# Split-weight buffers in the feed-forward blocks of a streaming encoder step: eleven slots in order of use instead of two big pairs and a ring of three

## The chip, the cores and the metric

The kernel runs on one core of a Trainium2 chip. Its engines are PE (the matrix engine, with PEld for its weight loads), DVE (vector), ACT (scalar), POOL (GpSimd) and SP, which here only issues DMA transfers. Every engine takes its instructions in the order in which they stand in its queue, and waits on semaphores for the others. The metric is the device time of one execution in microseconds (us).

## What is computed

One inference step of a two-layer encoder trunk: 512 frames of a new stream and 8 x 16 frames of running streams (640 columns in all), width 1024. Layer 0 is a convolution module, layer 1 is chunked attention over a shared K/V. Each is followed by a SwiGLU feed-forward block of hidden width 2816, and these two blocks are what the change touches.

```python
def swiglu_ffn(h, g, w_in, w_out):
    a, b = jnp.split(rms_norm(h, g) @ w_in, 2, axis=-1)
    return h + (jax.nn.silu(a) * b) @ w_out

def run_trunk(x, ...):                       # for the prompt and for the sample group
    for l in range(DEPTH):                   # DEPTH = 2
        if l < N_A_LAYERS:
            h, st = conv_module(h, ...)      # GLU, causal depthwise conv of width 31, LayerNorm, swish
        else:
            if l == N_A_LAYERS:
                k, v = jnp.split(rms_norm(h, norm_kv) @ w_kv, 2, axis=-1)
            q = rms_norm(h, norm_attn[j]) @ w_q[j]
            h = h + attention(q, k, v, rel_bias[j]) @ w_o[j]
        h = swiglu_ffn(h, norm_ffn[l], w_ffn_in[l], w_ffn_out[l])
    return rms_norm(h, norm_final), new_hist, k, v
```

All values are float32. The outputs are the two normed streams, the convolution buffers and the K and V rows.

## The kernel before

**Precision.** A float32 value is cut into a high and a low part, both of the matmul type fp32r: ACT copies the value (`hi`), DVE subtracts that copy from it (`lo`). In the feed-forward block `cut` (through `put`, lines 319 and 320) does this for weights. A product then takes three matmuls for each 128 x 128 piece of weights: hi by hi, lo by hi, hi by lo (`product`, line 379).

**Seven products.** `ffn` handles the 640 columns as two halves of 320 (`NH`) and the 1024 inputs as two halves as well. Of 22 blocks of the input matrix (128 gate and 128 value columns each), three (`w_std`, `std`) take the ordinary eight products. The other 19, and 12 blocks of the output matrix, take seven products instead of eight: the four quarters of a block's weights are added up in a fixed pattern (`w_seven`), the activations too (the tiles named X11 to X22), and each of the seven weight combinations meets one activation combination. A product of an input block has 12 matmuls (84 in a block), one of an output block has 9 (63 in a block). The order of work of a layer is: the three ordinary blocks, then three chunks, each of six input blocks (three in the first) followed by four output blocks (`out_chunk`), then four input blocks whose hidden values meet the rest of the output matrix (`w_out`) in ordinary products. In the text an *input block* and an *output block* are these, and an *out chunk* is the four output blocks.

**A block's way.** `w_seven` loads one block: SP issues the load of a 128 x 512 piece into `s1` and of the whole block (128 x 2048 floats, 1 MB; 1536 for an output block) into `raw`. POOL issues two DMAs that add another quarter onto `s1` and onto one quarter of `raw`. ACT and DVE cut the quarters and sums. PE uses the cut weights. `raw` and `s1` have two buffers each.

**Where cut weights stood.** The first four (X11, X21, XT2, XT1) stood together in one big pair `whi`, `wlo` of 2048 columns, of which there are two, used in turn by block. X11 and X21 were cut in one pass over 1024 columns (768 for an output block). The other three (XT3, XT4, X22) stood in a ring of three pairs `shi`, `slo` of 512 columns.

**What sets the order.** The tile framework's scheduler orders each engine's queue at build time, by the program's order and by priorities: weight cuts and the copies out of PSUM are marked as urgent (`tc.high_priority`). The products of an out chunk follow a string, `QORD`: in "51" the 5 is the product (`prod` in `out_chunk`) and the 1 the output block; "a0" and "a1" are the last two products (XT4 and X22) of the input block ahead, which `seven` hands on as `after`. So the last two products of each input block come after the first ones of the next block.

**Copies out of PSUM.** `keep` (line 388) is an ACT copy of a partial sum before the next product is added to the same PSUM tile, `plus` (line 393) is a DVE addition, and line 508 adds an output product to the residual `h` on DVE.

The lines that the prediction uses: 356 and 357 (SP loads of `s1` and `raw`), 361 and 362 (POOL's adding DMAs), 319 and 320 (cuts), 364 and 370 (sums of quarters on DVE), 379 (matmuls), 388 and 393 (copies and additions from PSUM), 604 (loads of `w_out`).

## Time and profile before

| what | value |
|---|---|
| three runs | 1534.5, 1539.4 and 3146.81 us; median 1539.4 us |
| the profiled execution | 1537.75 us, span 1535.9 us, granted TensorE clock 0.983 |
| PE busy | 1456.9 us (95%) |
| DVE busy | 1082.2 us (70%) |
| ACT busy | 739.7 us (48%) |
| feed-forward block of layer 0 | about 267 us to 676 us of the span; 326 to 664 us lies inside its seven-product part |
| feed-forward block of layer 1 | about 1082 us to 1517 us of the span; 1144 to 1478 us lies inside its seven-product part |

The rest of the span is the convolution module (up to 267 us) and attention (about 676 to 1082 us). A row of a wait list names who waited, on which line, and for whom, then the sum in us, the number of waits and the longest one. A row of a window list names a stretch of the span and then, by engine, busy time and number of instructions, after these the granted TensorE clock (1.00 is full) and the mean busy share of the DMA engines. Since matmuls overlap, the matrix engine counts as busy when it could have started another matmul: its busy share is no measure of how fast matmuls follow each other.

### The profile page before, as it was taken

The numbers are of one execution on the slowest core, as the hardware profiler recorded it, in microseconds if no ns is written. First come the engines' busy times: TensorE is split into PE (matmuls) and PEld (weight loads), VectorE is DVE, ScalarE is ACT, GpSimd is POOL, SyncE is SP. The second block draws the span as 40 slices with busy tenths as digits, with TensorE's granted clock in tenths as the row PEclk, the third lists the DMA queues.
The fourth block names the chain that finished last, engine by engine and source line by source line (L and its number), as shares of the span: only waits on it lengthen the run. The fifth ranks groups of instructions, "written<-read, shape, count | busy, mean of one in ns | idle before, by whom it ended". The sixth has DMA issues, their size and how long they took to land.

```text
span 1535.9 us, 28172 instructions
## 1 busy us (share of the span) xinstructions
PE 1456.9 (95%) x10974; PEld 1376.3 (90%) x10974; DVE 1082.2 (70%) x2357; ACT 739.7 (48%) x1555; POOL 337.9 (22%) x374
## 2 busy tenths in 40 slices
PE   5999899999999999999999999978999999999995
PEld 5998689999999999999887888957999999999994
DVE  5789346788688677676676666654788678688664
ACT  3666246453453553455564453542554454454442
POOL 5789222011111111113221121111001111111101
PEclk9999899999999999999999999998999999999997
DMA  7267414146655655534565455541235665665521
GB/s 235 63 188 181 100 56 137 42 97 146 155 136 142 157 134 127 152 117 146 189 190 189 139 173 192 172 154 42 69 72 136 152 149 127 156 147 134 146 90 69
DMA packets 79941, 207.25 MB, mean 135 GB/s; under 512 B 12992, under 2 KB 37312, under 8 KB 71360
## 3 DMA queue, kind: packets, MB, share of 16 engines
q1 hardware_dynamic: 61664, 175.78, 35.6%
q0 software_dynamic: 17856, 29.37, 12.5%
q8 instruction: 86, 1.41, 0.4%
q14 instruction: 47, 0.39, 0.1%
q10 hardware_dynamic: 288, 0.31, 0.1%
HBM read 193.82 MB, written 11.61 MB: 134 GB/s over the span
## 4 chain that ended last, share of the span: by engine, by line
PE 46%; DMA 22%; DVE 17%; ACT 6%; POOL 5%; issue 3%; SPq 0%; POOLq 0%; DVEq 0%; ACTq 0%
PE mm L379 13%; DMA raw<-in_w_in 9%; PE mm L167 8%; PE mm L168 7%; PE mm L169 7%; DMA raw<-in_w_os 6%; DVE wlo L320 4%; DMA s<-in_w_in 4%; POOL ca L726 4%; ACT whi L319 4%; DVE slo L320 3%; PE mm L764 2%; DVE raw L364 2%; DVE h L508 1%; PE w L203 1%
## 5 line engine op out<-in xcount | busy, mean ns | idle before, releaser
L379 PE MATMUL mm<-XH,whi 128*128 128x320 f32 x736 | 223.3, 312 | 8.9 <-ACT whi L319 8.9
L379 PE MATMUL mm<-XH,wlo 128*128 128x320 f32 x736 | 227.8, 311 | 1.3 <-DVE wlo L320 1.3
L379 PE MATMUL mm<-XL,whi 128*128 128x320 f32 x736 | 226.4, 310 | 0.0
L320 DVE TENSOR_TENSOR wlo<-raw,whi 128x1024 fp32r<-128x1024 f32 (+3 forms) x140 | 127.5, 917 | 124.1 <-ACT whi L319 123.9
L167 PE MATMUL mm<-xh,whi 128*128 128x320 f32 (+2 forms) x640 | 200.8, 316 | 4.3 <-ACT xh L156 2.6
L168 PE MATMUL mm<-xh,wlo 128*128 128x320 f32 (+2 forms) x640 | 200.0, 313 | 0.6 <-DVE wlo L151 0.6
L319 ACT ACTIVATE whi<-raw 128x1024 fp32r<-128x1024 f32 (+3 forms) x140 | 113.0, 814 | 178.5 <-DMA raw<-in_w_in 75.9
L169 PE MATMUL mm<-xl,whi 128*128 128x320 f32 (+2 forms) x640 | 197.1, 312 | 0.0
L379 PE MATMUL mm<-XH,shi 128*128 128x320 f32 x504 | 156.1, 310 | 3.7 <-ACT t L388 3.2
L379 PE MATMUL mm<-XH,slo 128*128 128x320 f32 x504 | 155.0, 308 | 0.0
L379 PE MATMUL mm<-XL,shi 128*128 128x320 f32 x504 | 154.4, 308 | 0.1
L379 PEld LDWEIGHTS mm<-XH,whi 128*128 128x128 f32 x736 | 137.1, 189 | 11.1 <-ACT whi L319 11.0
L319 ACT ACTIVATE shi<-raw 128x512 fp32r<-128x512 f32 (+1 forms) x192 | 110.9, 582 | 69.0 <-PE mm L379 61.4
L379 PEld LDWEIGHTS mm<-XH,wlo 128*128 128x128 f32 x736 | 138.8, 189 | 2.6 <-DVE wlo L320 2.4
L379 PEld LDWEIGHTS mm<-XL,whi 128*128 128x128 f32 x736 | 138.5, 189 | 0.0
L379 PE MATMUL mm<-hid,whi 128*128 128x320 f32 x576 | 135.2, 309 | 0.6 <-ACT whi L319 0.6
L320 DVE TENSOR_TENSOR slo<-raw,shi 128x512 fp32r<-128x512 f32 (+1 forms) x192 | 121.2, 635 | 11.3 <-ACT shi L319 10.8
L167 PEld LDWEIGHTS mm<-xh,whi 128*128 128x128 f32 x640 | 121.4, 190 | 7.8 <-ACT xh L156 3.1
L168 PEld LDWEIGHTS mm<-xh,wlo 128*128 128x128 f32 x640 | 121.7, 190 | 1.2 <-DVE wlo L151 0.8
L169 PEld LDWEIGHTS mm<-xl,whi 128*128 128x128 f32 x640 | 120.8, 190 | 1.2 <-issue 1.0
L379 PE MATMUL mm<-hid,shi 128*128 128x320 f32 x432 | 106.7, 312 | 2.9 <-ACT shi L319 1.6
L379 PEld LDWEIGHTS mm<-XH,shi 128*128 128x128 f32 x504 | 94.5, 187 | 6.2 <-ACT t L388 5.6
(228 smaller groups left out, 3503.3 us busy)
## 6 DMA issues: line engine op xcount, KB each, us to landing
raw<-in_w_in SPq DMA_DIRECT2D x38, 1024.0 KB
raw<-in_w_os SPq DMA_DIRECT2D x24, 768.0 KB
cache<-in_ck SPq DMA_DIRECT2D x32, 512.0 KB
cache<-in_cv SPq DMA_DIRECT2D x32, 512.0 KB
raw<-in_w_pw SPq DMA_DIRECT2D x12, 1024.0 KB
s<-in_w_in SPq DMA_DIRECT2D x38, 256.0 KB
s<-in_w_in POOLq DMA_DIRECT2D x38, 256.0 KB, 4.7
raw<-in_w_in POOLq DMA_DIRECT2D x38, 256.0 KB, 4.2
```

The costliest lines, as they stand in the source:

```text
L167: nc.tensor.matmul(ps, wh, xh, start=(i == 0), stop=False)
L168: nc.tensor.matmul(ps, wl, xh, start=False, stop=False)
L169: nc.tensor.matmul(ps, wh, xl, start=False, stop=(i == last))
L203: nc.tensor.matmul(st[:, 512 + t * w + k:513 + t * w + k], s[:, a:a + P], onec, start=True, stop=True)
L319: nc.scalar.activation(out=hi, in_=src, func=AF.Copy)
L320: nc.vector.tensor_tensor(out=lo, in0=src, in1=hi.bitcast(F32), op=sub)
L364: nc.vector.tensor_tensor(out=a11, in0=s1, in1=a11, op=add)
L379: nc.tensor.matmul(pt, wt, v, start=(first and k == i == 0), stop=(k == len(xs) - 1 and i == 2), skip_group_check=True)
L508: nc.vector.tensor_tensor(out=hv, in0=hv, in1=pt, op=sub if row else add)
L726: nc.gpsimd.tensor_tensor(out=acc, in0=acc, in1=pr, op=ALU.add)
L764: nc.tensor.matmul(pt[32 * q:32 * q + 32, 0:n], w4[0:r, 4 * tg + q, :], mv, start=(tg == 0), stop=(tg == 7))
```

## The change

In the feed-forward blocks the two big pairs are allocated once per layer, and the three ring pairs and the eight quarters of the big pairs make a list of eleven slots of 512 columns. `slot()` hands them out in turn. `w_seven` takes one slot per product, in the order in which the products use them, and cuts each product's weights by itself: X11 and X21 are now two passes of 512 columns (384 for an output block) where one pass of 1024 (768) was. The order of the cuts in an output block becomes XT1, X11, X21, XT2, X22, XT3, XT4. In `QORD` product 2 of output block 1 ("21") comes two places later, "61" and "70" change places, and so do "52" and "40". The ordinary blocks and `w_out` use the same memory as before, now by way of the list or of the fixed pairs. No arithmetic changes.

```diff
-QORD = "50 a0 10 a1 20 51 11 21 60 30 61 70 31 52 40 71 12 22 41 62 32 53 72 13 23 42 63 33"
+QORD = "50 a0 10 a1 20 51 11 60 30 21 70 61 31 40 52 71 12 22 41 62 32 53 72 13 23 42 63 33"
...
-        def wbig():
-            return [wp.tile([P, 2048], F32R, tag="w" + t, name=nm("w" + t)) for t in ("hi", "lo")]
-
-        def wring():
-            return [wx.tile([P, 512], F32R, tag="s" + x, name=nm("s" + x), bufs=3)
-                    for x in ("hi", "lo")]
+        wbig = [[wp.tile([P, 2048], F32R, tag="w" + t, name=nm("w" + t)) for t in ("hi", "lo")]
+                for _ in range(2)]
+        slots = [(wx.tile([P, 512], F32R, tag=f"shi{i}", name=nm("shi"), bufs=1),
+                  wx.tile([P, 512], F32R, tag=f"slo{i}", name=nm("slo"), bufs=1), 0)
+                 for i in range(3)]
+        slots += [(hi, lo, o) for hi, lo in wbig for o in range(0, 2048, 512)]
+        turn = [0]
+
+        def slot():
+            turn[0] += 1
+            hi, lo, o = slots[(turn[0] - 1) % len(slots)]
+            return (hi, lo), o
...
             n = src.shape[-1] // 4
-            raw, w = wraw(), wbig()
+            raw, ws = wraw(), {}
...
-            ws = {X11: (w, n), X21: (w, 0), XT2: (w, 2 * n), XT1: (w, 3 * n)}
             with tc.high_priority(offset=HP):
                 nc.gpsimd.dma_start(s1, src[:, 3 * n:4 * n], accum_op=add)
                 nc.gpsimd.dma_start(a21, src[:, n:2 * n], accum_op=add)
-                cut(w, 0, raw[:, :2 * n])
-                nc.vector.tensor_tensor(out=a11, in0=s1, in1=a11, op=add)
-                cut(w, 2 * n, a11)
-                cut(w, 3 * n, s1)
-                for x in (X22, XT3, XT4) if out else (XT3, XT4, X22):
-                    ws[x] = (wring(), 0)
-                    if x == X22:
+                for x in ((XT1, X11, X21, XT2, X22, XT3, XT4) if out else
+                          (X11, X21, XT2, XT1, XT3, XT4, X22)):
+                    if x == XT2:
+                        nc.vector.tensor_tensor(out=a11, in0=s1, in1=a11, op=add)
+                    elif x == X22:
                         nc.vector.tensor_tensor(out=a12, in0=a12, in1=a11, op=add)
-                    cut(*ws[x], {X22: a12, XT3: a21, XT4: a22}[x])
+                    ws[x] = slot()
+                    cut(*ws[x], {XT1: s1, X11: a11, X21: a12, XT2: a11, X22: a12, XT3: a21,
+                                 XT4: a22}[x])
             return ws
...
-            raw, w = wraw(), wbig()
+            raw, w = wraw(), wbig[m0 // 4]
```

What this does to the queues is shown at three places. The first is the ACT queue in layer 0, where two input blocks meet in the middle of the second chunk. Rows of line 319 are cuts (or, with `hid`, hidden values), `whi` and `shi` are slots, the number behind `raw` tells the blocks apart; lines 388 and 397 are a PSUM copy and a SiLU (392 and 401 after the change). In brackets are the semaphores that a row waits for: `DMAHW` is a load by SP, `DMASW` one of POOL's adding DMAs. Before:

```order
L319 ACTIVATE shi_599_4642<-raw_595_4627 128x512 [waits DMASW6_49,Activation_49]
L388 ACTIVATE t1_607_4669<-mm_605_4655 128x320 [waits PE_49]
L319 ACTIVATE hid_590_4581<-B01_580_4530 128x320 [waits DVE_49]
L319 ACTIVATE whi_614_4763<-raw_613_4762 128x1024 [waits DMAHW6_49]
L397 ACTIVATE t1_607_4669<-t1_607_4669 128x320 [waits DVE_49]
L319 ACTIVATE shi_601_4646<-raw_595_4627 128x512 [waits PE_49,Activation_49]
L319 ACTIVATE whi_614_4763<-raw_613_4762 128x512 [waits DVE_49]
L319 ACTIVATE hid_559_4393<-B00_608_4683 128x320 [waits DVE_49]
L319 ACTIVATE shi_603_4650<-raw_595_4627 128x512 [waits PE_49,Activation_49]
```

The ACT queue after the change, at the place that answers to it in the same chunk, where one input block follows another (`raw_525`, then `raw_535`):

```order
L319 ACTIVATE shi_325_2803<-raw_525_4696 128x512 [waits PE_49]
L319 ACTIVATE hid_487_4339<-B00_520_4617 128x320 [waits DVE_49]
L319 ACTIVATE whi_317_2795<-s1_526_4697 128x512 [waits DMASW7_49,PE_49]
L401 ACTIVATE t2_512_4537<-t2_512_4537 128x320 [waits DVE_49]
L392 ACTIVATE t2_522_4666<-mm_517_4589 128x320 [waits PE_49,Activation_49]
L319 ACTIVATE whi_317_2795<-raw_525_4696 128x512
L319 ACTIVATE whi_319_2797<-raw_535_4833 128x512 [waits DMAHW7_49,PE_49]
L319 ACTIVATE hid_490_4374<-B00_520_4617 128x320 [waits DVE_49]
L392 ACTIVATE t1_529_4732<-mm_527_4718 128x320 [waits PE_49]
L319 ACTIVATE shi_321_2799<-raw_535_4833 128x512 [waits DMASW1_49,Activation_49]
```

Before, the last two cuts of a block (of `raw_595`) stood behind the first cut of the next block, which waits for that block's load. After, all cuts of a block (`raw_525`) stand ahead of the first cut of the next one.

The second place is the SP queue in layer 0, from the first out chunk to the input blocks behind it. `s1` and `raw` are the two loads of a block, `in_w_os` are output blocks, `in_w_in` input blocks; a wait for DVE is one for the last cut or sum that read the buffer. Before:

```order
L357 DMA raw_490_3892<-in_w_os0 128x1536 [waits DMAHW4_49,DMASW6_49,DVE_49]
L356 DMA s1_519_4117<-in_w_os0 128x384 [waits DMASW7_49,DVE_49,Activation_49]
L357 DMA raw_503_4003<-in_w_os0 128x1536 [waits DMAHW2_49,DMAHW6_49,DMASW0_49,DVE_49]
L356 DMA s1_532_4218<-in_w_in0 128x512 [waits DMASW1_49,DMAHW3_49,DVE_49,Activation_49]
L357 DMA raw_516_4114<-in_w_os0 128x1536 [waits DMAHW0_49,DMASW2_49,DVE_49]
L356 DMA s1_548_4338<-in_w_in0 128x512 [waits DMAHW5_49,DMASW3_49,DVE_49]
L357 DMA raw_529_4215<-in_w_in0 128x2048 [waits DMAHW2_49,DMASW4_49,DVE_49]
L357 DMA raw_545_4335<-in_w_in0 128x2048 [waits DMAHW4_49,DMAHW7_49,DMASW6_49,DVE_49]
```

After (the loads of `raw` are on line 362 now, those of `s1` on line 361):

```order
L361 DMA s1_464_3984<-in_w_os0 128x384 [waits DMASW5_49,DVE_49]
L362 DMA raw_463_3983<-in_w_os0 128x1536 [waits DMAHW5_49,DMASW7_49,DVE_49]
L361 DMA s1_469_4079<-in_w_os0 128x384 [waits DMAHW2_49,DMASW1_49,DVE_49]
L362 DMA raw_468_4078<-in_w_os0 128x1536 [waits DMAHW3_49,DMAHW6_49,DMASW0_49,DVE_49]
L361 DMA s1_474_4174<-in_w_in0 128x512 [waits DMASW2_49,DVE_49]
L361 DMA s1_482_4288<-in_w_in0 128x512 [waits DMASW4_49,DVE_49,Activation_49]
L362 DMA raw_473_4173<-in_w_in0 128x2048 [waits DMAHW1_49,DMASW3_49,DVE_49]
L362 DMA raw_481_4287<-in_w_in0 128x2048 [waits DMAHW3_49,DMAHW7_49,DMASW5_49,DVE_49]
```

Each `raw` load still waits on DVE for its buffer. The loads of `s1` stand no longer strictly one block ahead: the one of the first input block (`s1_474`) now stands behind the load of the last output block (`raw_468`), where it stood ahead of it.

The third place is PE in the first out chunk of layer 0, where `slo`, `shi`, `whi`, `wlo` are the weight slots and `hid` the hidden values. Before:

```order
L379 MATMUL mm_475_3806<-hid_484_3868,shi_469_3793 128x320 [waits DVE_49]
L379 MATMUL mm_479_3835<-hid_482_3864,whi_466_3779 128x320 [waits DVE_49]
L379 MATMUL mm_501_3931<-hid_482_3864,whi_491_3893 128x320
L379 MATMUL mm_500_3920<-hid_397_3315,shi_494_3907 128x320 [waits Activation_49]
L379 MATMUL mm_479_3835<-hid_399_3320,shi_471_3798 128x320 [waits DVE_49]
```

After:

```order
L383 MATMUL mm_447_3811<-hid_450_3840,shi_325_2803 128x320 [waits DVE_49]
L383 MATMUL mm_461_3901<-hid_450_3840,whi_319_2797 128x320
L383 MATMUL mm_465_4005<-hid_389_3252,shi_325_2803 128x320 [waits Activation_49]
L383 MATMUL mm_466_4026<-hid_359_2950,whi_317_2795 128x320 [waits DVE_49]
```

Before, the cut into `shi_494` went into the ring slot that the first row here had read, with two matmuls between that row and the one that needs the new weights. After, the slot `shi_325` is read in the first row, written anew, and read again two rows later, with one matmul between. The matmul behind it no longer waits for a DVE addition into `h` that depends on the same first rows.

5 lines of the change are left out of this document (2 added, 3 removed).

## The prediction

> **What bounds the kernel now.** I read the busy line, then the chain that ended last, then the feed-forward stretches by windows, and last the waits in them.
>
> ```profile
> PE 1456.9 (95%) x10974; PEld 1376.3 (90%) x10974; DVE 1082.2 (70%) x2357; ACT 739.7 (48%) x1555; POOL 337.9 (22%) x374
> PE 46%; DMA 22%; DVE 17%; ACT 6%; POOL 5%; issue 3%; SPq 0%; POOLq 0%; DVEq 0%; ACTq 0%
> ...
> 326.00:664.00 338.00, 329.31 (x2209) 325.13 (x2208) 254.27 (x493) 164.29 (x321) 48.26 (x56) 0.99 0.56 140
> 1144.00:1478.00 334.00, 326.22 (x2193) 321.34 (x2192) 251.39 (x489) 161.23 (x317) 47.89 (x55) 1.00 0.57 140
> 386.00:389.20 3.20, 3.20 (x13) 3.20 (x14) 3.20 (x6) 1.78 (x3) 0.28 (x2) 0.50 0.93 266
> 390.00:450.00 60.00, 60.00 (x411) 60.00 (x410) 43.90 (x80) 32.20 (x65) 8.73 (x11) 1.00 0.56 136
> 477.00:592.00 115.00, 112.36 (x756) 110.87 (x756) 87.18 (x170) 56.42 (x111) 17.41 (x20) 1.00 0.58 144
> ```
>
> PE is the bound, yet the chain spends 22% in DMA: both lie close together. In the window rows PE comes first (busy, matmuls), then PEld, DVE, ACT, POOL, the granted clock and the DMA share. From 390 to 450 us PE is never short of work: 60.00 us / 411 = 0.146 us per matmul. At that pace the 2209 matmuls of the first long stretch need 322.5 of its 338 us and the 2193 of the second 320.2 of 334 us. So **15.5 + 13.8 = 29.3 us** are lost where the change works, and this is the most that it can win there: 1.9% of 1537.75 us.
>
> The waits behind that, layer 0 and then layer 1 (sum, number, longest):
>
> ```profile
> PE mm L379 <- ACT whi L319: 5.6, 5, 1.9
> PE mm L379 <- ACT t L388: 1.3, 3, 0.7
> PE mm L379 <- ACT shi L319: 1.0, 3, 0.4
> PE mm L379 <- DVE h L508: 0.6, 2, 0.4
> ...
> PE mm L379 <- ACT whi L319: 3.9, 4, 1.4
> PE mm L379 <- DVE wlo L320: 1.3, 2, 0.8
> PE mm L379 <- ACT t L388: 1.3, 4, 0.4
> PE mm L379 <- ACT shi L319: 0.6, 2, 0.4
> PE mm L379 <- DVE h L508: 0.6, 2, 0.4
> ```
>
> These are 16.2 us in 27 waits. A wait costs more than its row: a matmul is shown for 0.31 us and the next could start after 0.146, so 0.165 us per wait are hidden in it, and the matmul behind a wait follows after about 0.25 us (361.21 to 361.46 below), another 0.10. With 0.265 x 27 = 7.2 us the sum is 23.4. The stretch at half clock (13 matmuls in 3.2 us, where 21.9 fit) costs another 1.3. The remaining 4.6 us I can't place, and leave as they are.
>
> The long waits are for a load. The chain, in order of time (start, length, what):
>
> ```profile
> 513.81 0.61 DVE slo L320
> ...
> 514.43 5.83 DMA raw<-in_w_in
> ...
> 520.28 1.07 ACT whi L319
> ...
> 521.38 1.22 DVE wlo L320
> ...
> 526.21 0.61 DVE slo L320
> ...
> 526.84 5.35 DMA raw<-in_w_in
> ...
> 537.16 7.15 DMA raw<-in_w_in
> ```
>
> The last ring cut of one block frees `raw`, the load follows, then its cuts, and ring cuts again: a round of 526.84 - 514.43 = 12.4 us, where PE needs 84 x 0.146 = 12.3 us for an input block. Two `raw` buffers work like one, for the reason that the ACT rows ahead show: the last ring cuts of a block stand behind the first cut of the next, which waits for its own load. In an out chunk PE needs only 63 x 0.146 = 9.2 us per block, so it eats up the lead there and waits at the first input block behind:
>
> ```profile
> 385.81 1.11 PE L379 MATMUL mm<-XH,whi 128*128 128x320 f32 x3 [1.90 <-ACT whi L319]
> ...
> 500.94 0.71 PE L379 MATMUL mm<-XH,whi 128*128 128x320 f32 x3 [1.42 <-ACT whi L319]
> ...
> 617.97 0.71 PE L379 MATMUL mm<-XH,whi 128*128 128x320 f32 x3 [1.56 <-ACT whi L319]
> ```
>
> **The change part by part.** *Slots in order of use.* A ring cut waited for the same product of the block ahead, 7 products back; a slot now waits for the one 11 products back. I followed every wait back through the queues of both built programs, SP, POOL and the semaphores included, to the last matmul that it depends on. From the matmul that a `raw` load depends on to the first product that uses the load there were 54 matmuls at the least, 81 in the median; now 80 and 171. In time: 54 x 0.146 = 7.9 us, 80 x 0.146 = 11.7 us. What must fit is the load (5.35 to 7.15 us) and a cut of 1.07 us, so 6.4 to 8.2 us: too close before, over 3 us to spare now. So the whi and wlo waits go: 5.6 + 3.9 + 1.3 = 10.8 us in 11 waits, with 0.265 each 13.7 us. With the first of them goes the half clock, 1.3 us. The t waits are copies out of PSUM that stand on ACT behind a cut which waits for its load; none but one per layer (below) is now within 12 matmuls of what it depends on. They go: 2.6 us in 7 waits, with the addition 4.5 us. What is late next is PE's own pace.
>
> *The out chunk's cut.* One wait stays, at the place of the PE rows ahead:
>
> ```profile
> 360.63 0.52 ACT L319 ACTIVATE shi<-raw 128x384 fp32r<-128x384 f32 x1 [1.39 <-PE mm L379]
> ...
> 361.21 0.56 PE L379 MATMUL mm<-hid,shi 128*128 128x320 f32 x2 [0.38 <-ACT shi L319]
> 361.46 0.19 PEld L379 LDWEIGHTS mm<-hid,slo 128*128 128x128 f32 x1
> ```
>
> The cut can begin only when PE has left the slot, and with one matmul between instead of two PE waits 0.146 us longer: 6 places, +0.9 us. The h waits behind it (1.2 us in 4 waits, 2.3 with the addition) go, as that addition now depends on a matmul 11 places back at four of the six places (3 and 7 at the others) instead of 2.
>
> *More, shorter instructions.* 38 input and 24 output blocks get one more pass on ACT and on DVE:
>
> ```profile
> L319 ACT ACTIVATE whi<-raw 128x1024 fp32r<-128x1024 f32 x54 | 56.3, 1056 | 91.4 <-DMA raw<-in_w_in 75.9 <-DMA raw<-in_w_out 9.3 <-PE mm L379 4.9
> L319 ACT ACTIVATE shi<-raw 128x512 fp32r<-128x512 f32 x120 | 73.8, 620 | 18.3 <-PE mm L379 14.3 <-PE am L1086 3.6
> L320 DVE TENSOR_TENSOR wlo<-raw,whi 128x1024 fp32r<-128x1024 f32 x54 | 65.4, 1224 | 92.3 <-ACT whi L319 92.2
> L320 DVE TENSOR_TENSOR slo<-raw,shi 128x512 fp32r<-128x512 f32 x120 | 81.8, 685 | 5.4 <-ACT shi L319 5.3
> L319 ACT ACTIVATE whi<-raw 128x768 fp32r<-128x768 f32 x24 | 20.3, 846 | 45.3 <-DMA raw<-in_w_os 45.3
> L319 ACT ACTIVATE shi<-raw 128x384 fp32r<-128x384 f32 x72 | 37.1, 519 | 50.7 <-PE mm L379 47.1 <-DVE raw L370 3.4
> L320 DVE TENSOR_TENSOR wlo<-raw,whi 128x768 fp32r<-128x768 f32 x24 | 23.0, 958 | 31.8 <-ACT whi L319 31.7
> L320 DVE TENSOR_TENSOR slo<-raw,shi 128x384 fp32r<-128x384 f32 x72 | 39.3, 553 | 5.9 <-ACT shi L319 5.5
> ```
>
> ACT: 2 x 620 - 1056 = 184 ns and 2 x 519 - 846 = 192 ns, so 38 x 0.184 + 24 x 0.192 = 11.6 us. DVE: 146 and 148 ns, so 9.1 us. I cost them at nothing: in the two long stretches DVE is idle for 84 and 83 us, ACT for over 170 each, and PE's work hides them; without that cover it would be all 20.7 us.
>
> [...]
>
> *The end of each layer.* The two `w_out` blocks now go into slots that the last input block still uses. In the built program a PSUM copy (t) stands 2 matmuls behind what it depends on, worth an average t wait with its addition (1.3 / 3 + 0.165 = 0.6 us), and a 1024-wide cut has 14 matmuls, 2.04 us, for 0.165 + 1.06 + 1.22 = 2.45 us. Together 1.0 us per layer, 2.0 in all. Nothing of this is in the trace of before: from below 0, if the copies run ahead, up to both cuts in full, 2 x 2 x (1.06 + 1.22) = 9 us. I take 2.0, as other t waits are that short.
>
> *Loads beside each other.* An earlier `raw` load can run beside others. At the DMA share of 0.56 that costs nothing; if two shared evenly, 5.35 us would become 10.7, with the cuts (0.62 + 0.69) 12.0 against 11.7: 0.3 us at 6 places. From 0 to 2 us, and I take 0. The moved entries of `QORD` are in the counts above; the SP and POOL queues were followed with them. Convolution and attention keep their order.
>
> **Sum.** 13.7 + 1.3 + 4.5 + 2.3 = 21.8 us gone, 0.9 + 2.0 = 2.9 us new: 18.9 us. 1537.75 - 18.9 = **1519 us**, 1.2% less. The profiled time lies 1.65 us below the median of the runs shown (1539.4). About 2% is what a measurement of this kernel can tell from no change.
>
> **A second look at the half clock.** The trace has it once, after the longest wait (1.90 us), and not after 1.42 us at 500.94 (clock 1.00 from 477 to 592).
>
> [...]
>
> **The rivals.**
> *Slower: slots make ACT wait for PE.* Eleven slots in strict turn mean that every cut stands on ACT until PE has left its slot, and the PSUM copies behind it are late. The row for it, from all of the kernel:
>
> ```profile
> ACT shi L319 <- PE mm L379: 61.4, 41, 4.0
> ```
>
> If each of 62 blocks took one wait like that of the out chunk (0.38 + 0.265 = 0.65 us), that is 40 us against the 21.8: **1556 us**; it turns slower from 34 blocks on. Against it: in the built program only one copy per layer comes that close.
> *No change: the loads set the pace anyway.* If the DMA engines, at 0.93 from 386 to 389 us, can't bring blocks earlier, or the 20.7 us of passes stand on the path after all (1537.75 - 18.9 + 20.7 = 1540), only the h waits go: 1537.75 - 2.3 = **1535 us**. Against it: the share of 0.56.
> *More: all loss goes*, the unplaced too: 1537.75 - 29.3 = **1508 us**. Against it: the out chunk's wait.
>
> **How the numbers follow.** Forecast (1513 to 1526 us) 0.58, more (below 1513) 0.12, no change (1526 to 1540) 0.18, slower (above 1540) 0.12. The range 1509 to 1537 us leaves out a third of "more", a sixth of "no change" and "slower", 0.19 in all, and takes in the bounds of the open costs (1517 to 1526). Beyond 2% lie about 1508.6 and 1570 us: faster 0.06 (half of "more"), slower 0.04 (a third of "slower"), the same 0.90.
>
> **What would show it.** Right: whi waits for line 319 at the first input block behind each out chunk gone, the clock at 1.00 from 386 us on, PE's 2209 and 2193 matmuls in about 10 us less each; ACT waiting for PE rather than for `raw`; shi or whi waits of 0.5 us at six out chunks. Wrong: PE waiting for t copies in many blocks, or `raw` loads that take 10 us.

## The result, and the profile after

Over 16 runs each, the kernel after ran 1543.8 us in the median and the kernel before 1540.3 us. The ratio of after to before is **1.0005, with a 95% interval from 0.9983 to 1.0027**: no change that can be measured. The profiled execution after has a span of 1539.5 us, where before had 1535.9. The forecast was 1519 us.

The page's busy line and its chain that ended last, after:

```profile
PE 1460.8 (95%) x10974; PEld 1381.9 (90%) x10974; DVE 1089.1 (71%) x2419; ACT 746.1 (48%) x1617; POOL 337.4 (22%) x374
...
PE 69%; DVE 10%; DMA 9%; POOL 5%; ACT 3%; issue 3%; SPq 0%; POOLq 0%; DVEq 0%; ACTq 0%
```

By this chain the change did what was forecast: DMA fell from 22% to 9%, DVE from 17% to 10%, PE rose from 46% to 69%. Yet the time is the same. So I looked at stretches, as before (busy time and number of instructions by engine, granted clock, DMA share, GB/s):

```profile
326.00:664.00 338.00, 332.51 (x2240) 329.48 (x2239) 259.89 (x529) 167.98 (x354) 48.86 (x56) 0.99 0.58 143
386.00:389.20 3.20, 3.20 (x24) 3.20 (x23) 2.91 (x7) 1.92 (x4) 0.40 (x1) 1.00 0.68 109
...
1144.00:1478.00 334.00, 324.80 (x2180) 321.78 (x2179) 252.33 (x513) 163.16 (x342) 47.97 (x55) 0.99 0.58 141
514.00:524.00 10.00, 7.36 (x40) 6.87 (x39) 5.79 (x11) 4.69 (x10) 1.68 (x2) 0.83 0.52 133
1216.00:1226.00 10.00, 6.88 (x47) 6.62 (x46) 6.93 (x14) 3.04 (x7) 1.76 (x2) 1.00 0.49 93
1332.00:1342.00 10.00, 6.55 (x28) 6.29 (x27) 6.32 (x12) 4.93 (x10) 1.73 (x2) 0.66 0.63 110
```

From 386 to 389 us, where before 13 matmuls ran at half clock, 24 run now. Over the two long stretches, though, PE does 2240 + 2180 matmuls instead of 2209 + 2193: 18 more, 2.6 us gained at 0.146 us each. The last three rows show where the rest went. At full pace 68 or 69 matmuls fit in 10 us; here are 40, 47 and 28. These **three stalls cost 4.2 + 3.1 + 5.9 = 13.2 us**, part of it at half clock. Before, PE's longest wait in these layers was 1.90 us; now they are 1.85, 3.12 and 3.45.

The three in order of time, with the transfers ahead of the first (start, length, engine, line, operation; in brackets the idle time before it and who ended it):

```profile
503.21 0.33 SPq L362 DMA_DIRECT2D raw<-in_w_in  x1
...
508.89 0.87 POOL L366 DMA_DIRECT2D raw<-in_w_in  x1 [9.16 <-DVE h L512]
...
509.62 0.33 SPq L362 DMA_DIRECT2D raw<-in_w_in  x1
...
516.76 0.63 ACT L319 ACTIVATE whi<-raw 128x512 fp32r<-128x512 f32 x1 [7.72 <-issue]
517.29 0.61 ACT L319 ACTIVATE whi<-s 128x512 fp32r<-128x512 f32 x1
517.42 0.69 DVE L320 TENSOR_TENSOR wlo<-raw,whi 128x512 fp32r<-128x512 f32 x1 [7.83 <-ACT whi L319]
...
517.96 0.42 PE L383 MATMUL mm<-XH,whi 128*128 128x320 f32 x1 [1.85 <-ACT whi L319]
...
1218.94 0.69 DVE L370 TENSOR_TENSOR raw<-s,raw 128x512 f32<-128x512 f32 x1 [7.30 <-DMA s<-in_w_in]
1219.55 0.48 DVE L397 TENSOR_TENSOR t<-mm,t 128x320 f32<-128x320 f32 x1
...
1220.08 0.41 PE L383 MATMUL mm<-XH,shi 128*128 128x320 f32 x1 [3.12 <-DVE t L397]
...
1334.32 0.63 ACT L319 ACTIVATE whi<-raw 128x512 fp32r<-128x512 f32 x1 [8.35 <-DMA raw<-in_w_in]
...
1335.38 0.42 ACT L392 ACTIVATE t<-mm 128x320 f32<-128x320 f32 x1
...
1335.85 0.64 PE L383 MATMUL mm<-XH,whi 128*128 128x320 f32 x1 [3.45 <-ACT t L392]
```

Read the first from the bottom. PE waits for the cut at 517.29, the XT1 cut (from `s1`) of one block. Its slot was free from 510.98 us, when the last matmul that read it ended. But ahead of it in ACT's queue stood the cut at 516.76, of the next block: it reads the third quarter of `raw` (XT3), onto which POOL's adding DMA of line 366, issued at 508.89, adds, and this DMA landed at 516.69. (`issue` in this row means that the view names nobody for the wait.) So ACT stood still for 7.7 us with work behind it. The third stall is the same, with a PSUM copy (line 392) behind the cut. In the second, DVE's addition of line 370 waits 7.3 us for the other adding DMA, on `s1`, and the addition that PE needs (line 397) stands behind it. Work of DVE did not hold these DMAs up: DVE itself stood idle for 7.8, 7.3 and 8.2 us up to the ends of the three waits.

The order in ACT's queue is new. In the built program before, no cut of a block stands behind the next block's cut of the third quarter, in 60 pairs of neighbouring blocks; after, in 23 of the 60 at least one does. The place in ACT's queue that is shown ahead of the prediction, where all cuts of a block stand ahead of the next one's, holds for 32 of the 60 pairs.

Who waited for the adding DMA on the block's quarter, and its time from issue to landing. Before (line 362), where nobody waited:

```profile
who waited for it (us, times):
...
DMA to landing us min/median/max: 3.6/4.2/6.5
```

After (line 366):

```profile
who waited for it (us, times):
  ACT whi L319: 24.0, 11
  ACT shi L319: 13.7, 7
...
DMA to landing us min/median/max: 3.6/4.2/7.8
```

The same for the other adding DMA, on `s1`, before (line 361) and then after (line 365):

```profile
who waited for it (us, times):
  ACT whi L319: 20.4, 17
...
DMA to landing us min/median/max: 3.6/4.8/7.9
```

```profile
who waited for it (us, times):
  DVE raw L370: 11.5, 4
  ACT whi L319: 2.6, 2
...
DMA to landing us min/median/max: 3.6/4.7/8.7
```

So late adding DMAs are not new: of 124, 9 took over 6.5 us before and 7 after. Late are above all those that are issued within 0.9 us of a load of `raw`. Before there are 23 of them, with a median of 6.3 us from issue to landing, where the other 101 have 4.2; after there are 10, with 6.3 against 4.2 again. What is new is what stands behind a late one.

ACT's waits for weight transfers, of all of the kernel, before and then after (sum, number, longest):

```profile
ACT whi L319 <- DMA raw<-in_w_in: 75.9, 31, 4.8
...
ACT whi L319 <- DMA raw<-in_w_os: 45.3, 22, 3.3
...
ACT whi L319 <- DMA s<-in_w_in: 19.6, 16, 2.2
```

```profile
ACT whi L319 <- DMA raw<-in_w_in: 44.7, 15, 8.3
...
ACT shi L319 <- DMA raw<-in_w_in: 23.4, 8, 7.1
...
...
ACT whi L319 <- issue: 16.0, 3, 7.7
...
ACT whi L319 <- DMA raw<-in_w_os: 14.0, 10, 2.8
```

They became fewer, and the longest nearly twice as long (8.3 us where it was 4.8; the wait of the first stall stands under `issue`). Most of these waits cost PE nothing: before, the three rows come to 140.8 us, where all waits of PE on line 379 come to 17.1. It was long ones, of 7.7 and 8.3 us, that used up PE's lead at the first and the third stall.

### The profile page after: what moved, and what is told of

It is laid out like the page before. It is cut to its first block, busy times and chain, and to the rows that moved or that the text cites. A ratio compares the mean times of both kernels' runs of the same rounds, so it can differ in the third digit from the quotient of the medians.

```text
span 1539.5 us, 28370 instructions
## 1 busy us (share of the span) xinstructions
PE 1460.8 (95%) x10974; PEld 1381.9 (90%) x10974; DVE 1089.1 (71%) x2419; ACT 746.1 (48%) x1617; POOL 337.4 (22%) x374
## 4 chain that ended last, share of the span: by engine, by line
PE 69%; DVE 10%; DMA 9%; POOL 5%; ACT 3%; issue 3%; SPq 0%; POOLq 0%; DVEq 0%; ACTq 0%
PE mm L383 36%; PE mm L167 7%; PE mm L168 7%; PE mm L169 7%; POOL ca L730 4%; DMA raw<-in_w_in 3%; DVE wlo L320 2%; PE mm L768 2%; DMA raw<-in_w_os 2%; DMA s<-in_w_in 2%; PE w L203 2%; PE am L1090 1%; PE w L1105 1%; DVE h L512 1%; PE am L1136 1%
## 5 line engine op out<-in xcount | busy, mean ns | idle before, releaser
L383 PE MATMUL mm<-XH,whi 128*128 128x320 f32 x896 | 277.7, 312 | 6.9 <-ACT t L392 4.0
L383 PE MATMUL mm<-XH,wlo 128*128 128x320 f32 x896 | 278.7, 311 | 0.8 <-DVE wlo L320 0.8
L383 PE MATMUL mm<-XL,whi 128*128 128x320 f32 x896 | 275.7, 311 | 0.0
L319 ACT ACTIVATE whi<-raw 128x512 fp32r<-128x512 f32 (+2 forms) x280 | 166.1, 611 | 179.6 <-PE mm L383 89.4
L320 DVE TENSOR_TENSOR wlo<-raw,whi 128x512 fp32r<-128x512 f32 (+2 forms) x280 | 184.0, 670 | 62.4 <-ACT whi L319 61.8
L383 PEld LDWEIGHTS mm<-hid,whi 128*128 128x128 f32 x732 | 124.7, 188 | 4.7 <-ACT whi L319 3.0
L383 PE MATMUL mm<-hid,wlo 128*128 128x320 f32 x366 | 111.5, 308 | 0.0
L383 PE MATMUL mm<-XH,shi 128*128 128x320 f32 x344 | 106.2, 309 | 4.1 <-DVE t L397 3.7
L383 PE MATMUL mm<-XH,slo 128*128 128x320 f32 x344 | 105.8, 308 | 0.0
L730 POOL TENSOR_TENSOR ca<-ca,cvt 128x512 f32<-128x512 f32 x60 | 91.2, 1520 | 14.9 <-ACT cvt L727 8.0
```

Source lines behind the costliest of these rows:

```text
L319: nc.scalar.activation(out=hi, in_=src, func=AF.Copy)
L320: nc.vector.tensor_tensor(out=lo, in0=src, in1=hi.bitcast(F32), op=sub)
L383: nc.tensor.matmul(pt, wt, v, start=(first and k == i == 0), stop=(k == len(xs) - 1 and i == 2), skip_group_check=True)
L730: nc.gpsimd.tensor_tensor(out=acc, in0=acc, in1=pr, op=ALU.add)
```

## The experiments

From these traces, theory A: ACT and DVE wait at the head of their queues for adding DMAs that land late, and hold up what PE needs. Rival B: the additional passes, or the slots, pace the kernel. Rival C: the loss lies outside the feed-forward layers. Beside the median of the runs the table has a measure that is free of what happens elsewhere: the time of both feed-forward layers in the profiled execution, from the first matmul of each to a fixed one near its end (of the core's 10974 matmuls in order of start the 2159th to the 4871st, and the 8111th to the 10811th), and the rest of the span. The scheduler orders the queues anew for each kernel; between e1 and the kernel after, PE's order differs in a tenth of its rows. All in us; the ratio is to the kernel before, run on the same chip, with its 95% interval.

| kernel | run, median | ratio | both layers | rest |
|---|---|---|---|---|
| before | 1540.3 | 1 | 821.3 | 714.6 |
| after | 1543.8 | 1.0005 [0.9983, 1.0027] | 818.8 | 720.7 |
| after again (e4) | 1541.1 | 1.0003 [0.9979, 1.0027] | 822.2 | 720.5 |
| after, short adding DMAs (e1) | 1519.1 | 0.9877 [0.9838, 0.9916] | 800.8 | 714.4 |
| after, additions on GpSimd (e2) | 1521.9 | 0.9898 [0.9861, 0.9935] | 803.4 | 716.8 |
| after, XT3 in the last slot (e3) | 1539.4 | 1.0011 [0.9985, 1.0037] | 820.9 | 715.0 |
| e2 with traffic, loose (e5) | 1647.1 | 1.0685 [1.0641, 1.0729] | not comparable | |
| before, additions on GpSimd (e6) | 1550.3 | 1.0056 [1.0028, 1.0083] | 826.1 | 718.1 |
| before, cuts in halves (e7) | 1542.1 | 1.0001 [0.9979, 1.0023] | 821.6 | 714.0 |
| after, old order (e8) | 1554.4 | 1.0076 [1.0049, 1.0104] | 833.3 | 719.3 |
| e2 with traffic, tied (e9) | 1527.5 | 0.9910 [0.9878, 0.9943] | 805.7 | 720.9 |
| after, GpSimd adds the quarter (e10) | 1531.5 | 0.9943 [0.9924, 0.9963] | 812.9 | 716.8 |
| after, GpSimd adds s1 (e11) | 1533.8 | 0.9952 [0.9933, 0.9972] | 812.1 | 715.7 |
| after, loads in halves (e12) | 1542.4 | 1.0006 [0.9986, 1.0027] | 826.7 | 714.1 |
| after, loads behind adding DMAs (e13) | 1526.1 | 0.9879 [0.9838, 0.9920] | 804.7 | 719.7 |
| before, short adding DMAs (e14) | 1523.6 | 0.9873 [0.9842, 0.9904] | 801.7 | 719.0 |
| before, loads behind adding DMAs (e15) | 1597.9 | 1.0354 [1.0309, 1.0399] | 879.4 | 715.4 |

**e1, short adding DMAs.**

```diff
-                nc.gpsimd.dma_start(s1, src[:, 3 * n:4 * n], accum_op=add)
-                nc.gpsimd.dma_start(a21, src[:, n:2 * n], accum_op=add)
+                nc.gpsimd.dma_start(s1[:, :32], src[:, 3 * n:3 * n + 32], accum_op=add)
+                nc.gpsimd.dma_start(a21[:, :32], src[:, n:n + 32], accum_op=add)
```

> The changed kernel, but the two adding DMAs of a block carry 32 of their 512 (or 384) columns, so part of the computation is left out (the sums X11+X22 and X21+X11 of a weight block are right in 32 columns only). Every wait stays, and the instructions stay nearly in place; only the time from issue to landing of these 124 DMAs falls (4.2 us in the median and up to 8.7 us now; I expect about 2 to 3 us). Theory A, that ACT's and DVE's queue heads wait for adding DMAs which land late beside the next block's 1 MB load, and hold up the copies and cuts that PE needs: the stalls at 518, 1220 and 1336 us of the changed kernel go, 14 to 15 us with their half clock, so 1523 to 1531 us. Rival B, that the 62 more passes on ACT and DVE or the slots pace the kernel: 1538 to 1545 us as now. Rival C, that the loss lies outside the feed-forward blocks, in windows at half clock that come and go: as now too, and the three stalls are either still there or were never worth their length.

1519.1 us, below the range of theory A: the layers are 18 to 21 us shorter than in the two profiles of after, which is more than the three stalls. (That it is also the time forecast for the change is a coincidence.) The two long stretches, and the landing of the DMA of line 366:

```profile
326.00:664.00 338.00, 336.31 (x2291) 335.10 (x2291) 264.13 (x533) 174.30 (x358) 48.93 (x56) 1.00 0.36 106
1144.00:1478.00 334.00, 332.19 (x2242) 330.71 (x2242) 254.95 (x513) 165.29 (x337) 44.45 (x51) 1.00 0.35 102
```

```profile
DMA to landing us min/median/max: 2.2/2.4/5.4
```

PE is busy for 668.5 of 672 us, with the same passes on ACT and DVE as in the kernel after. This rules out that the passes or the slots as such pace the kernel (rival B). It does not tell a wait for these DMAs from their traffic, as their bytes go too: the DMA share fell from 0.58 to 0.36.

**e4, the kernel after once more.**

> The changed kernel once more, unaltered. Theory A: the three stalls of 2 to 4 us come back at the same places (518, 1220, 1336 us), since they follow from the order of the queues; the time lies within 0.3% of the kernel before. Rival C: the stalls move or are gone in this profile and the time of the convolution and the attention (the half clock at 180 to 190 us and 1018 to 1064 us) moves by several us.

The three stalls came back (gaps between two matmuls of 2.37, 3.33 and 4.71 us at 517, 1221 and 1339 us), so they belong to the program. Both theories held in part: the rest of the span is 6 us above before in both profiles of after, with the same instructions in it. How much the rest varies is told further down.

**e7, the price of the passes alone.**

```diff
-                    n = 512 if small else 1024
+                    n = 512
...
-                cut(w, 0, raw[:, :2 * n])
+                cut(w, n, a11)
+                cut(w, 0, a12)
```

> The kernel before with only its 1024-wide cuts (768 in output blocks) made in two halves, so it has the 62 more passes of the changed kernel on ACT (11.6 us) and DVE (9.1 us) in the old buffers. Theory A: hidden beside PE, 1536 to 1544 us. Rival B, the passes stand on the path: 1550 to 1560 us.

1.0001, in theory A's range: in the old buffers the 62 more passes cost nothing that can be measured, as forecast. (With this edit there are 70 on each engine, as the ordinary blocks get 8 more.)

**e2 and e6, both additions on GpSimd**, in the kernel after and in the kernel before:

```diff
-            nc.sync.dma_start(s1, src[:, 2 * n:3 * n])
...
-                nc.gpsimd.dma_start(s1, src[:, 3 * n:4 * n], accum_op=add)
-                nc.gpsimd.dma_start(a21, src[:, n:2 * n], accum_op=add)
+                nc.gpsimd.tensor_tensor(out=s1, in0=a21, in1=a22, op=add)
+                nc.gpsimd.tensor_tensor(out=a21, in0=a21, in1=a11, op=add)
```

> The changed kernel with both additions done by GpSimd from the block in SBUF (two tensor_tensor on POOL in place of the load of s1 and the two adding DMAs): the whole computation, with 1.0 MB per input block instead of 1.75 MB from memory. Theory A: ACT's and DVE's waits for in_w_in and in_w_os behind these DMAs go, 1518 to 1528 us, which would beat both kernels. Rival B (passes or slots): 1538 to 1545 us. Rival D, that POOL's additions (two of 512 columns per block, 62 blocks) come later than the DMAs or slow DVE down: above 1545 us.

> The kernel before (old buffers, old order) with both additions on GpSimd. Theory A: a raw load still depends on ring cuts, 54 matmuls at the least ahead of its first product, so the whi waits behind each out chunk stay, a little shorter as the loads run alone (5.35 to 7.15 us would become about 5): 1528 to 1537 us, and the eleven slots are worth the 7 to 15 us from there to 1522. Rival E, that the slots are worth nothing even then and all of the gain of the GpSimd version is the adding DMAs': 1519 to 1525 us.

With the slots 1521.9 us, in theory A's range, 1.0% less than before and with the whole computation; with the old buffers 1550.3, slower than before, which neither theory had. There ACT waits for DVE (sum, number, longest; before it was 40.2 us in 36 waits):

```profile
ACT whi L319 <- DVE raw L363: 73.2, 57, 2.6
```

DVE was slower for it: its `wlo<-s,whi` pass of 512 columns took 1315 ns in e6 where it took 687 before. That this is all of what e6 lost is not shown.

**e5 and e9, the traffic put back without the waits.** e5 added copies that wait for nothing:

> The kernel with both additions on GpSimd, and three idle transfers per weight block put back: parts of the block are copied from memory to a scratch in memory that nothing reads, 3 x 256 KB per input block (192 KB per output block), one issued by SyncE and two by GpSimd, as the load of s1 and the adding DMAs were. So the bytes are those of the changed kernel, but no cut waits for them. Theory A1, that the harm was that ACT and DVE wait in their queues for the adding DMAs: 1520 to 1527 us, as without the transfers. Theory A2, that the traffic as such makes the raw loads late: 1533 to 1542 us.

They all ran at the very start, before the blocks they belong to (from 49 to 162 us of its span PE was busy for 7.4 us), so e5 says nothing on the question. In e9 the copies read what GpSimd has added, so they stay with their block:

```diff
                 nc.gpsimd.tensor_tensor(out=s1, in0=a21, in1=a22, op=add)
                 nc.gpsimd.tensor_tensor(out=a21, in0=a21, in1=a11, op=add)
+                for d in dm:
+                    nc.gpsimd.dma_start(d, a21)
```

> As the kernel with both additions on GpSimd, with traffic put back in another way than before: once GpSimd has added, it copies that quarter of the block three times to a scratch in memory that nothing reads (3 x 256 KB per input block), so the transfers cannot run ahead of their block, the bytes per block are again 1.75 MB, and nothing but the next load into that buffer depends on them. Theory A1 (the harm was the wait for the adding DMAs): 1519 to 1528 us. Theory A2 (traffic as such makes the raw loads late): 1532 to 1545 us.

1527.5 us, the layers 805.7 us against 803.4: with all the bytes, but no work waiting for the transfers, the layers lose 2.3 us; the kernel after loses 15 to 19. This speaks for A1. It does not close the question: the copies bring back the bytes (142 to 145 GB/s in the two long stretches), but they keep the DMA engines less busy than the adding DMAs do (share 0.41 to 0.42 against 0.58).

**e3 and e12, the order turned at one place each.** e3 gives XT3, the cut that stood at ACT's head, the last slot of its block; e12 loads first the half onto which the DMA adds:

```diff
-                          (X11, X21, XT2, XT1, XT3, XT4, X22)):
+                          (X11, X21, XT2, XT1, XT4, X22, XT3)):
```

> The changed kernel with one order turned: in the input blocks the cut of the sum that the adding DMA makes (product XT3) takes the last of the block's seven slots instead of the fifth, so it can start about two products, some 24 matmuls or 3.5 us, later, and less stands behind it on ACT. Theory A: the two stalls in which ACT's head was this cut (518 and 1336 us) shrink or go, the one on DVE (1220 us) stays: 1528 to 1536 us. Rivals B and C: 1538 to 1545 us.

```diff
-            nc.sync.dma_start(raw[:, :4 * n], src)
+            for i in (2 * n, 0):
+                nc.sync.dma_start(raw[:, i:i + 2 * n], src[:, i:i + 2 * n])
```

> The changed kernel with the same bytes, but each load of a weight block in two halves, the half first that the adding DMA adds to, so that it can start about 2.5 us earlier. Theory A1: ACT's waits for this DMA shrink, 1528 to 1537 us. Theory A2 and B: 1537 to 1545 us.

Both expectations of theory A missed: no gain, and both times lie in the ranges of the rivals. In e12 ACT's waits for the quarter's DMA did fall, from 37.7 to 24.7 us, but DVE's waits for the other, on `s1`, rose from 11.5 us in 4 to 29.4 in 6. My picture of one cut at the wrong place was too narrow: there are two such DMAs per block, and either is enough.

**e10 and e11, one of the two at a time** (only the second, or only the first line of e2's change; e11 without the load of `s1`):

> The changed kernel with only one of the two adding DMAs done by GpSimd: that on a quarter of the loaded block (the one that ACT waits for in 18 places and 37.7 us). The other (on s1) stays a DMA. Theory A1: the stalls at 518 and 1336 us go, the one on DVE at 1220 us (behind s1) may stay or come at another place: 1522 to 1533 us. Theory A2: 1533 to 1541 us, as only a seventh of the bytes goes.

> The other half alone: s1 by GpSimd, without its load and its adding DMA (1.25 MB per block instead of 1.75), while the adding DMA on the block's quarter stays. Theory A1: ACT's waits for that DMA stay, a little shorter, 1525 to 1536 us, so slower than the version that does only the other. Theory A2: faster than that one, as twice the bytes go, 1522 to 1529 us.

Each brings part of it (layers 812.9 and 812.1 us, where the kernel after has 818.8 and 822.2 and e2 803.4), and the one that stays is waited for more: 30.8 us by DVE in e10 (11.5 in the kernel after), 61.2 us by ACT in e11 (37.7). This agrees with the reading of e12, and both times lie in the ranges of theory A1. Which of the two is worth more isn't told apart (1531.5 and 1533.8, overlapping intervals).

**e13 and e15, the loads behind the adding DMAs, with the same bytes**, in after and in before:

```diff
-            nc.sync.dma_start(raw[:, :4 * n], src)
+            nc.gpsimd.dma_start(raw[:, :4 * n], src)
```

> The changed kernel with the raw loads issued by GpSimd instead of SyncE, in one queue with the adding DMAs, so that the load of a block stands behind the adding DMA on the block ahead of it in most places (in two of each layer's rounds two loads still stand ahead of both). The bytes are the same. Theory G, that an adding DMA lands late because the next block's load runs beside it: the longest landing of the DMA on the block's quarter falls from 7.8 us to under 6 us and ACT's wait for it from 37.7 us to 15 to 25 us; the feed-forward blocks get 3 to 12 us shorter, unless the s1 DMA, which now stands behind other waits in POOL's queue, takes that back: 1528 to 1541 us. Rival, that they are late by themselves: landings as now, 1538 to 1548 us.

> The kernel before (old buffers) with the raw loads issued by GpSimd, behind the adding DMA on the block ahead in most places; same bytes. Theory H, that one cause (transfers beside each other) made both the waits for raw loads before and those for adding DMAs after: 1522 to 1533 us, about the changed kernel with its loads moved so (1526). Rival I, that with full adding DMAs the old buffers' short distance still costs its whi waits, and the slots are needed: 1534 to 1543 us.

e13: 1526.1 us, 1.2% less, the whole computation, all 1.75 MB per block. Its windows and the landing of line 366:

```profile
326.00:664.00 338.00, 333.71 (x2265) 331.22 (x2264) 260.32 (x530) 169.51 (x357) 63.45 (x82) 1.00 0.56 142
1144.00:1478.00 334.00, 331.20 (x2240) 329.18 (x2239) 256.97 (x519) 166.77 (x345) 61.44 (x80) 1.00 0.55 140
```

```profile
  ACT whi L319: 29.2, 15
  ACT shi L319: 15.1, 7
...
DMA to landing us min/median/max: 3.5/4.1/6.3
```

The DMA share is 0.56 and 0.55, where the kernel after has 0.58, so it is not the bytes. What the edit changes is the order in which the transfers stand, and with it when the loads start. Of the 62 DMAs on a block's quarter, 3 took over 6.5 us in the kernel after; in e13 none did. Of those on `s1` it is 3 where it was 4, the longest 7.1 us instead of 8.7. And the 19 adding DMAs that are issued within 0.9 us of a load take 4.5 us in the median here, where the 10 in the kernel after took 6.3: beside a load that stands in the same queue they are hardly late. Three numbers of the expectation missed: the time lies below the range (the layers are 14 to 17.5 us shorter, 3 to 12 were expected), the longest landing was to fall under 6 us and is 6.3, and ACT's wait for this DMA was to shrink and rose to 44.3 us, as DVE's for the one on `s1` rose, from 11.5 to 27.1 us. The sums of the waits are not the measure; the longest ones are what became shorter, and PE's longest wait in the two stretches fell from 3.5 to 1.5 us.

Why an adding DMA takes longer beside a load in SyncE's queue (6.3 us in the median) than beside one in its own (4.5 us), no run shows.

In e15 the same edit makes the old buffers 3.5% slower, far outside both ranges: the layers take 58 us more. Counted in matmuls, 46 of the 62 loads of `raw` now start later, by 24 matmuls at most, and PE's waits on the whi cuts grow (all of the kernel):

```profile
PE mm L379 <- ACT whi L319: 31.4, 12, 5.8
```

Theory H fell. With the loads so late the slots are worth 75 us, which fits their longer distance from load to product; where the 58 us come from, beyond these waits, was not worked out.

**e14, the kernel before with short adding DMAs** (the edit of e1).

> The kernel before with adding DMAs of 32 columns, as in the first experiment (the same part of the computation is left out). Theory A, that the slots are worth about what was forecast once the adding DMAs are short: the whi waits for raw loads stay, as they don't depend on these DMAs, 1532 to 1541 us, 13 to 22 us above the changed kernel with the same DMAs. Rival E, that short DMAs alone bring it all: 1518 to 1526 us.

The rival was right, and I was not: 1523.6 us, the layers 801.7 us against 800.8 with the slots. Once the adding DMAs are short, the slots are worth 0.9 us of the 18.9 forecast for them. At the wait of 1.90 us before the matmul at 385.81, the load was issued at 379.14 and its cut began at 384.70, 5.6 us later, with the adding DMA on `s1` issued beside it at 379.74; in e14 it was 380.33 and 385.18, 4.9 us, and the wait 0.38 us. So the load that PE waited for before was itself late by 0.7 us because of an adding DMA beside it. The other 0.8 us come from the load ahead of it, in the same way: from its issue to its first cut it took 6.2 us (366.51 to 372.73) and takes 5.4 in e14 (368.51 to 373.93), with an adding DMA on `s1` issued 3 us behind it that landed after 4.7 and now after 2.6 us; from that cut to the issue of the next load it is 6.4 us in both. The orders of PE, SP and POOL are the same in both programs, so the two places can be set side by side. It holds beyond this place: for input blocks, where ACT stood waiting for the load, the time from a load's issue to its first cut is 5.7 us in the median before and 5.0 in e14, and PE's whi waits in the two long stretches fall from 9.5 us in 9 to 2.9 in 6, with the distance of 54 matmuls unchanged:

```profile
PE mm L379 <- ACT whi L319: 1.2, 3, 0.4
...
PE mm L379 <- ACT whi L319: 1.7, 3, 0.8
```

**e8, the slots with the old order.** With it the XT4 product of each chunk's first output block (entry "40") comes behind "52", whose cuts already overwrite its slot, so it reads another block's weights. This is why the change moves entries of `QORD`.

```diff
-QORD = "50 a0 10 a1 20 51 11 60 30 21 70 61 31 40 52 71 12 22 41 62 32 53 72 13 23 42 63 33"
+QORD = "50 a0 10 a1 20 51 11 21 60 30 61 70 31 52 40 71 12 22 41 62 32 53 72 13 23 42 63 33"
```

> The changed kernel's eleven slots with the old order of the output products. Theory A: the order of the out chunk hardly matters for the three stalls; one of its cuts has to wait for a product that is now directly ahead of it, 1538 to 1548 us. Rival F, that the new order is what costs (it moves the additions of an output block): 1525 to 1533 us.

1554.4 us, above both ranges: the new order is not what costs (rival F fell), the layers take 11 to 14.5 us more without it. Where those come from I did not follow up.

**The four pairs together** (both layers, us):

| transfers | old buffers | eleven slots | slots are worth |
|---|---|---|---|
| as they were | 821.3 | 818.8 and 822.2 | -1 to 2.5 |
| adding DMAs short | 801.7 | 800.8 | 0.9 |
| additions on GpSimd | 826.1 | 803.4 | 22.7 |
| loads behind the adding DMAs | 879.4 | 804.7 | 74.7 |

The fastest kernels with the whole computation are e2 and e13, with 1.0% and 1.2% less than before; their intervals overlap. Both need the slots: the same edits in the old buffers (e6, e15) made them slower.

## Why the prediction was wrong

The change stayed within 2%, as forecast, but the time was wrong: 1519 us, with a range up to 1537, against 1543.8. Of the 25 us between them 2.5 are the base (the sum starts from 1537.75 us, the median of before is 1540.3), 3.5 the difference of the two medians, which the interval does not tell from nothing, and 18.9 the gain that did not come.

- **"What must fit is the load (5.35 to 7.15 us) and a cut of 1.07 us, so 6.4 to 8.2 us: too close before, over 3 us to spare now."** This step failed. The distance was counted from a load's cause to the first product that uses the load. Behind the load comes an adding DMA, behind that a cut or an addition that waits for it in the queue, and behind these the work that other products need. Counted through that (same queues, same program), the distance did not grow: from the matmul that a load depends on to the first product that stands behind the adding DMA there were 120 matmuls at the least for input blocks and 125 for output blocks; now there are 114 and 97. (The second stall hangs on the adding DMA on `s1`: from the matmul that this one depends on to the first product behind it there are 103 for input blocks, at the least, before and after.) At the first stall there are 124 from the matmul at 497.40 to the one at 517.96, 18.1 us at PE's pace. What must fit is: 5.8 us until the load is issued (503.21), 5.7 until the adding DMA is (508.89), 7.9 until the cut behind it starts (516.76), and 1.2 for this cut, the next and the matmul, 20.6 us. With an adding DMA at its median of 4.2 us it would be about 17 and fit. The other half of the step, that 54 matmuls were too few before, was right for loads that have an adding DMA beside them; in e14 the same 54 are all but enough (2.9 us in 6 waits are left).
- **"Loads beside each other ... from 0 to 2 us, and I take 0."** The term that was mis-sized. "At the DMA share of 0.56 that costs nothing" is an average over 338 us; the three stalls, 13.2 us, come where a 1 MB load and an adding DMA are issued within 0.9 us of each other (load 509.62 and DMA 508.89; 1210.05 and 1210.16; 1325.80 and 1326.69). The sum set the load's own length against the load's own distance, and had no term for the adding DMA. The slots did not make such pairs more frequent (23 before, 10 after); with them, work that PE needs soon stands behind the late DMA.
- **"They go" (the t waits).** Not so. Of 7 small ones before, 4 of 0.3 to 0.5 us are left (3 of them for DVE's addition), and two of the three stalls are waits for t, because the copy or addition stood behind a late DMA.
- **Right: the whi waits** behind each out chunk went, and with them the half clock at 386 us (granted clock 1.00 from 386.0 to 389.2 us, 0.50 before). **The out chunk's cut**: forecast was 0.146 us more at each of six places; the gap between two matmuls is 0.77 us at five and 0.90 at one, where it was 0.69 at the first before, so 0.08 more there. **The end of each layer**: a t wait worth 0.6 us was forecast, and both gaps there are 0.60 us, 0.45 above the pace; the 0.4 us for a wide cut is not told apart. (The sum adds 0.165 us to this wait and 0.265 to every other one; the difference is 0.2 us.) **The passes at nothing**: e7.
- **The half clock, "1.3 us" gone**: gone there, and back at two of the new stalls (clock 0.83 and 0.66 in the windows above).
- **The rivals.** "No change: the loads set the pace anyway" named the side of it, DMA, and gave 1535 us, but for the wrong transfers, and it was given 0.18. By its classes 1543.8 us is "slower (above 1540)", but so is the kernel before with 1540.3; the ratio of 1.0005 is no change. That the time stayed within 2% (0.90) came about in another way than forecast, and that it hardly moved is luck: the whi waits went, 15.0 us with their half clock by the prediction's sum, and 13.2 us of new stalls came. "Slower" by waits for slots did not show.
- **What remains open**: e2, e9 and e13 together say that waiting for late adding DMAs is the harm and not their bytes, but none of them keeps all of the traffic and its timing; of the sixteen completion marks of the DMA of the first stall, fifteen had come by 514.91 us and the last at 516.69, and why is not known; the 11 to 14.5 us of e8 and most of the 58 of e15.

## What to carry over

When a buffer is deepened, follow the distance through every transfer of the block and through what stands behind its first reader in each in-order queue, not only from the load to its own product; the shortest such way counts. The mean DMA share of 0.56 to 0.58 over the long stretches did not show that adding DMAs issued within 0.9 us of a load took 6.3 us in the median, and the others 4.2. And before a gain is booked to more buffers, ask what made the wait as long as it was: here transfers beside each other made most of it (PE's whi waits in the two long stretches were 9.5 us, and 2.9 with short adding DMAs). Shortening them brought the gain without the new buffers (layers 801.7 us in e14, 821.3 before); ordering them did so only with these (804.7 us in e13, 879.4 in e15).

## What the runs showed of the hardware

**The time at half clock differs from run to run.** The sixteen runs of the kernel after had granted clocks from 0.975 to 0.984, and times from 1532.9 to 1547.4 us. Outside the feed-forward layers all kernels run the same instructions, but for the `w_out` blocks, yet the rest of the span in the table goes from 714.0 to 720.9 us. It follows the time at half clock in the convolution and the attention, by the clock records from 20.5 us (e7: 714.0) and 23.9 us (e1: 714.4) to 41.0 us (e9: 720.9), in stretches of 3.4, 6.8 or 10.2 us. Both profiles of after have about 6 us more there than the one of before (37.5 us at half clock in both, and 27.3 in before). Other kernels with the slots lie on both sides (23.9 us in e1 and e12, 41.0 in e9), so I don't book it to the change; that it is chance is not shown. Whether a stretch at half clock follows a wait in these layers is not told by the wait's length here: behind the one of 1.90 us before there is one (clock 0.83 from 384 to 394 us), behind 3.12 us at 1220.08 after there is none (1.00 from 1216 to 1226 us), and behind the same wait in the second profile of after, 3.0 us, there is (0.83 from 1217 to 1227 us).

**In e2, DVE's passes are slower beside GpSimd's additions.** DVE's pass `wlo<-raw,whi`, the kernel after and then e2, where GpSimd adds:

```profile
L320 DVE TENSOR_TENSOR wlo<-raw,whi 128x512 fp32r<-128x512 f32 x162 | 109.5, 689 | 46.9 <-ACT whi L319 46.5
```

```profile
L320 DVE TENSOR_TENSOR wlo<-raw,whi 128x512 fp32r<-128x512 f32 x162 | 142.1, 893 | 8.4 <-ACT whi L319 7.6
```

The same 162 instructions take 893 ns instead of 689. In e2, 96 of them run while GpSimd adds nothing and take 683 ns in the mean; the 66 that overlap one of its additions take 1197 ns. With the slots there is room for it (in e2 DVE is busy for 297.8 of 338 and 287.1 of 334 us in the two long stretches), and e2 is faster; in the old buffers (e6) ACT's waits for DVE grew, and that this used up what the missing DMAs gave is likely but not measured.
